# Projection tiles issued behind each batch of an S5 scan, and eight gate tiles per layer computed there and kept in HBM

## The chip, the cores and the metric

One Trainium2 chip (trn2), one core of it. The metric is the device time of one execution in microseconds. The kernel before took a median of 1589.26 us in three runs (1584.7 to 1589.46). Its five engines are called PE (TensorE), DVE (VectorE), ACT (ScalarE), POOL (GpSimd) and SP (SyncE, which here issues nearly all DMAs).

## What is computed

One inference step of a two-layer backbone over 640 tokens (512 latent, 128 context) of width 1024. What matters here of one layer:

```python
h = rms_norm(x) * (1 + scale) + shift
u_a, g_a, u_b, g_b, u_c, g_c, m = split(h @ w_in)
y_a = s5_glu(u_a) * silu(g_a)          # 32 groups x 16 channels, scans in both directions
y_b = hyena(u_b) * silu(g_b)           # two long convolutions by FFT
y_c = multipool(u_c) * silu(g_c)       # centred means over 2, 4, 8, 16 positions
m_a, m_b, m_c = split(sigmoid(m))
merged = m_a * (y_a @ w_br_a) + m_b * (y_b @ w_br_b) + m_c * (y_c @ w_br_c)
x = x + gate * (merged @ w_out)
```

The combined projection `h @ w_in` has 56 column tiles of 128 columns. Of these 0 to 3 are u_a, 4 to 7 g_a, 8 to 19 u_b, 20 to 23 g_b, 24 to 27 u_c, 28 to 31 g_c, and 32 to 55 the merge gates of the three branches, eight each.

## The kernel before

**A projection tile.** `win(l, nt, cb)` computes one of the 56 tiles for all 640 tokens by `linear` (L248 to L259). Both operands are kept as a rounded high part and a low part, and three products make up one: for two weight chunks of 128 x 512, each loaded by SP (tile `wr`, three slots), ACT writes the high part `wh` (L234) and DVE the low part `wl` (L235). For both halves of 320 tokens and eight blocks of 128 rows PE runs three matmuls (L257, L258, L259), 48 in all, into one `mm` buffer of PSUM for each half (three slots). `cb(half, ps)` takes the finished half out of PSUM.

**Merge tiles in pairs.** The merge tiles of branches b and c (40 to 55) are computed two at a time by `win2`, with seven products of a 2 x 2 block scheme where the plain way has eight: 7 x 12 = 84 matmuls for two tiles (L329 to L331). It needs four weight loads, sums of weights on POOL (L314 to L317), seven weight splits, five additions on DVE and two on POOL (L335). Its prepared operands `thi` and `tlo` are made by `win2_prep` (L282), on DVE, during the merges of branch a.

**The order of one layer** in the program (`layer`, then `merges`):

1. `u_a`: four tiles, written to HBM and read back regrouped (`load_u`).
2. Eight batches of the S5 scan. `s5_gen` builds a batch's operands: tables on DVE, POOL and ACT, transposes (L864) and small products (L884) on PE, and a kernel `kd` that goes to HBM and comes back as `mt` in eight pieces. `s5_run` does PE products (L929, L931), the rotation and scans on DVE (L938 to L953, the scans are L946 and L947), output products on PE (L959, L961) and a GELU (L965 to L969) whose result goes to HBM.
3. Twelve Hyena input tiles (`conv_u`): a projection tile copied by ACT into a padded tile `raw` (two slots, L982), then a three-tap filter by one ACT (L987) and two DVE instructions (L989, L991).
4. Four gate tiles of branch b (`gate_b`): a projection tile with a Silu on ACT (L998), and a POOL product (L1006).
5. `glu`: four tiles of g_a, and the GLU of branch a.
6. Four Hyena calls (`hyena`). Each has a loop over four residues `r`: transform on PE (`xf`), products on DVE (L1101, L1102), sums on POOL (L1103, L1104), a split on ACT and DVE, and behind the loop the inverse transforms (L1117). Behind each call stands one `pool_branch`, with a projection tile of u_c (L1017) and one of g_c through `silu_tile` (tile `sgc`, L998), and behind the third and fourth call two merges of branch a each (`merge`: a plain projection tile with a Tanh, L1189, then `branch`, a product with `w_br` and an accumulation, L1211 and L1213).
7. `merges`: the other four merges of branch a, the preparation of `win2`, then for branches b and c four calls of `merge2`: one `win2` and two `branch` calls each. In layer 0 the modulation products of the next step (L400) stand between them.

**What sets the order on the engines.** The program is written in a tile framework with a scheduler of its own (`TileContext(nc, schedule_with_timeline_sim=True)`): it knows the buffers and the data, and orders each engine's instructions by a model of the time. Each engine then works off its queue in order; so does SP with its DMAs.

## Time and profile before

| | |
|---|---|
| three runs, us | 1584.7, 1589.26, 1589.46 |
| profiled execution: span from first to last instruction, us | 1583.7 |
| busy: PE, PE weight loads, DVE, ACT, POOL (share of the span) | 92%, 88%, 74%, 41%, 44% |
| mean granted TensorE clock | 0.951 |
| HBM read, written, MB | 150.12, 21.56 |

The profiled execution is given by its span, 1583.7 us; what lies around the span (start and end of the program) is not part of it, and the lowest of the three runs is 1.0 us above it. Busy times count an engine's own instructions, not its waits nor the issue of DMAs. The granted clock is the share of TensorE's full clock that it was given, 1.00 being 2.4 GHz. In the views "x" is a count, "<-" stands between what an instruction writes and what it reads, and an arrow behind an idle time names what ended it.

### The profile page before, as it was taken

The page shows a single profiled execution, that of the slowest core. Times are in us where ns is not written, and L with a number is a line of the kernel's source. Part 1 is how long each engine was busy: PE and PEld are TensorE (multiplying, and loading weights), DVE is VectorE, ACT ScalarE, POOL GpSimd, SP SyncE. Part 2 cuts the span into 40 slices and gives each one's busy share as a digit, 9 for nine tenths or more (in the row PEclk, how much of TensorE's full clock was granted, in tenths as well). Part 3 has the DMA queues.
Part 4 walks back from the last instruction along what each step waited for, and adds up shares of the span by engine and source line. Part 5 has one row for each costly group of instructions (what it writes and reads, how often), then busy time and mean ns, then how long its engine had stood idle before and what let it go on. Part 6 is the DMA issues. An engine that isn't in the chain of part 4 may idle for free.

```text
span 1583.7 us, 28484 instructions
## 1 busy us (share of the span) xinstructions
PE 1460.2 (92%) x10764; PEld 1390.7 (88%) x10764; DVE 1179.0 (74%) x1964; ACT 645.1 (41%) x1330; POOL 690.9 (44%) x704
## 2 busy tenths in 40 slices
PE   4888887899999999999998878889999999999997
PEld 2568887799999998999997878889999999999996
DVE  6689999965777795555677799998377769766565
ACT  3274333324333443444335543333443334444443
POOL 5926465630344325454322646654115243566411
PEclk8689888999999999999999998889999999999999
DMA  9425212234222334553552431222532213222154
GB/s 319 164 81 124 68 53 61 61 89 142 91 80 79 102 104 150 180 170 139 190 180 89 123 100 53 64 61 70 152 96 75 81 61 120 81 81 83 41 169 154
DMA packets 114945, 173.53 MB, mean 110 GB/s; under 512 B 30360, under 2 KB 54568, under 8 KB 114297
## 3 DMA queue, kind: packets, MB, share of 16 engines
q1 hardware_dynamic: 113433, 165.37, 33.4%
q0 software_dynamic: 1296, 6.19, 1.1%
q8 instruction: 85, 1.39, 0.3%
q14 instruction: 51, 0.42, 0.1%
q10 hardware_dynamic: 80, 0.16, 0.0%
HBM read 150.12 MB, written 21.56 MB: 108 GB/s over the span
## 4 chain that ended last, share of the span: by engine, by line
PE 64%; DVE 19%; issue 5%; POOL 4%; DMA 3%; SPq 2%; ACT 2%; POOLq 0%; DVEq 0%; ACTq 0%
PE mm L259 13%; PE mm L258 13%; PE mm L257 13%; PE mm L329 4%; PE mm L331 4%; PE mm L330 4%; DVE wl L235 2%; PE modp L400 2%; DVE i L854 1%; PE inva L1117 1%; PE invb L1117 1%; DVE i L853 1%; DVE vx L989 1%; DVE kk L947 1%; DVE kk L946 1%
## 5 line engine op out<-in xcount | busy, mean ns | idle before, releaser
L257 PE MATMUL mm<-hhi,wh 128*128 128x320 f32 x1280 | 405.1, 318 | 10.8 <-ACT raw L982 6.9
L259 PE MATMUL mm<-hhi,wl 128*128 128x320 f32 x1280 | 404.9, 319 | 9.5 <-DVE wl L235 9.4
L258 PE MATMUL mm<-hlo,wh 128*128 128x320 f32 x1280 | 404.7, 317 | 4.4 <-DVE hlo L661 3.6
L235 DVE TENSOR_TENSOR wl<-wr,wh 128x512 fp32r<-128x512 f32 x312 | 256.2, 823 | 90.1 <-ACT wh L234 86.7
L234 ACT CAST wh<-wr 128x512 fp32r<-128x512 f32 x312 | 192.6, 618 | 250.6 <-PE mm L258 181.2
L257 PEld LDWEIGHTS mm<-hhi,wh 128*128 128x128 f32 x1280 | 247.2, 193 | 14.4 <-ACT raw L982 7.9
L259 PEld LDWEIGHTS mm<-hhi,wl 128*128 128x128 f32 x1280 | 246.8, 193 | 12.9 <-DVE wl L235 11.9
L258 PEld LDWEIGHTS mm<-hlo,wh 128*128 128x128 f32 x1280 | 247.5, 193 | 6.5 <-DVE hlo L661 4.5
L258 PE MATMUL mm<-mlo,wh 128*128 128x320 f32 x256 | 79.7, 312 | 0.5 <-DVE mlo L238 0.4
L329 PE MATMUL mm<-hhi,wh 128*128 128x320 f32 x256 | 79.9, 312 | 0.0
L331 PE MATMUL mm<-hhi,wl 128*128 128x320 f32 x256 | 79.5, 311 | 0.0
L257 PE MATMUL mm<-mhi,wh 128*128 128x320 f32 x256 | 79.0, 312 | 0.5 <-ACT wh L234 0.5
L259 PE MATMUL mm<-mhi,wl 128*128 128x320 f32 x256 | 78.9, 310 | 0.4 <-DVE wl L235 0.4
L330 PE MATMUL mm<-hlo,wh 128*128 128x320 f32 x256 | 79.2, 309 | 0.0
L235 DVE TENSOR_TENSOR wl<-ws,wh 128x512 fp32r<-128x512 f32 x64 | 54.4, 849 | 32.1 <-ACT wh L234 30.8
L1211 DVE SCALAR_TENSOR_TENSOR mth<-mth,mm 128x320 f32<-128x320 f32 x64 | 31.2, 488 | 54.8 <-PE mm L259 54.8
L234 ACT CAST wh<-ws 128x512 fp32r<-128x512 f32 x64 | 39.7, 620 | 72.8 <-PE mm L330 36.9
L335 DVE TENSOR_TENSOR mth<-mm,mth 128x320 f32<-128x320 f32 x80 | 39.2, 491 | 33.8 <-PE mm L331 17.2
L961 PE MATMUL yp<-w,ow 128*128 128x81 f32 x256 | 45.5, 307 | 17.5 <-DVE w L953 17.4
L331 PE MATMUL mm<-thi,wl 128*128 128x320 f32 x192 | 60.7, 316 | 0.0
L329 PE MATMUL mm<-thi,wh 128*128 128x320 f32 x192 | 60.6, 316 | 0.0
L330 PE MATMUL mm<-tlo,wh 128*128 128x320 f32 x192 | 59.4, 309 | 0.0
(420 smaller groups left out, 4069.0 us busy)
## 6 DMA issues: line engine op xcount, KB each, us to landing
wr<-w_in SPq DMA_DIRECT2D x224, 256.0 KB
wm<-w_mod SPq DMA_DIRECT2D x48, 512.0 KB
wr<-w_out SPq DMA_DIRECT2D x48, 256.0 KB
hd<-hs SPq DMA_DIRECT2D x32, 256.0 KB
hsr<-hd SPq DMA_DIRECT2D x32, 256.0 KB
mt<-kd SPq DMA_DIRECT2D x128, 32.0 KB
wr<-w_br_a SPq DMA_DIRECT2D x16, 256.0 KB
wr<-w_br_b SPq DMA_DIRECT2D x16, 256.0 KB
```

What stands on the lines that cost most here:

```text
L234: nc.scalar.copy(hi, src)
L235: nc.vector.tensor_tensor(out=lo, in0=src, in1=hi.bitcast(F32), op=ALU.subtract)
L257: nc.tensor.matmul(ps[i], wh[:, ks], at(hi, k, sl), start=(k == 0), stop=False)
L258: nc.tensor.matmul(ps[i], wh[:, ks], at(lo, k, sl), start=False, stop=False)
L259: nc.tensor.matmul(ps[i], wl[:, ks], at(hi, k, sl), start=False, stop=(k == kt - 1))
L329: nc.tensor.matmul(out, wh[:, ks], xh, start=(k == 0), stop=False)
L330: nc.tensor.matmul(out, wh[:, ks], xl, start=False, stop=False)
L331: nc.tensor.matmul(out, wl[:, ks], xh, start=False, stop=(k == 3))
L335: e.tensor_tensor(out=o, in0=x, in1=y, op=ALU.add)
L400: nc.tensor.matmul(ps[r0:r0 + 32, :], self.cs[:, 2 * hf + q, :], w[:, q, :], start=(hf < 2), stop=(hf >= 2))
L961: nc.tensor.matmul(yp[:, cols], ow[:, r, g].rearrange("p t h -> p (t h)"), w[:, r, g, 0:CW], start=False, stop=(r == 1))
L1117: nc.tensor.matmul(out, yy[:, ri, cs], ww, start=(n == 0), stop=(n == 5))
```

## The change

Behind each of the eight scan batches of a layer three projection tiles are issued, from a list `beside` in this order: the twelve Hyena tiles, the four gate tiles of branch b, four tiles 28 to 31 (g_c, Silu) and four tiles 40 to 43 (merge gates of branch b, Tanh of half the value). The last eight are new there. `ahead` computes such a tile by `win`, puts its activation into a slot of the tag `raw`, and stores it to a tile `gd` in HBM by an SP DMA of 320 KB. Where the tile was computed before, it is now read back by an SP DMA: in `silu_tile` for the pooling branch, and in `merge2` for its first two calls of branch b, which then call no `win2`. The order of the final-state DMA (`ns`) and the tiles changes accordingly.

```diff
--- before.py
+++ after.py
@@ -219,7 +219,7 @@
 class Body:
     def __init__(self, nc, tc, I, O, dbg=None):
         self.nc, self.tc, self.I, self.O, self.dbg = nc, tc, I, O, dbg or {}
-        self.smod, self.sacc = {}, {}
+        self.smod, self.sacc, self.gd = {}, {}, {}
 
     def dump(self, name, ap):
         if name in self.dbg:
@@ -991,8 +991,22 @@
         nc.vector.scalar_tensor_tensor(out=o, in0=raw[:, 2:644], scalar=cw[:, 3 * i + 2:3 * i + 3], in1=o,
                                        op0=ALU.mult, op1=ALU.add)
 
+    def ahead(self, l, nt, func, scale, U):
+        nc = self.nc
+        st = U.tile([P, L642 + 2], F32, tag="raw", name="gst", bufs=2)[:, 0:T]
+
+        def cb(half, ps):
+            nc.scalar.activation(st[:, half * HT:half * HT + HT], ps, func, scale=scale)
+
+        self.win(l, nt, cb)
+        self.gd[l, nt] = self.DR.tile([P, T], F32, name=f"gd{l}_{nt}")
+        nc.sync.dma_start(self.gd[l, nt], st)
+
     def silu_tile(self, l, nt, dst):
         nc = self.nc
+        if (l, nt) in self.gd:
+            nc.sync.dma_start(dst[:, 0:T], self.gd[l, nt])
+            return
 
         def cb(half, ps):
             nc.scalar.activation(dst[:, half * HT:half * HT + HT], ps, AF.Silu)
@@ -1193,7 +1207,12 @@
 
     def merge2(self, l, n, br, ys):
         ths = [self.M.tile([P, 644], F32, tag="t", name="mth", bufs=4)[:, 0:T] for _ in range(2)]
-        self.win2(l, 32 + 8 * br + n, ths)
+        nt = 32 + 8 * br + n
+        if (l, nt) in self.gd:
+            for i in range(2):
+                self.nc.sync.dma_start(ths[i], self.gd[l, nt + i])
+        else:
+            self.win2(l, nt, ths)
         for i in range(2):
             self.branch(l, n + i, br, ys, ths[i])
 
@@ -1370,14 +1389,16 @@
             uas = [SP.tile([P, NT, CW], F32, name=f"ua{i}") for i in range(2)]
             self.u_a(l, S, uas)
             self.load_u(l, S)
+            beside = [lambda i=i: self.conv_u(l, i, vx[i // 4][:, i % 4, :], SP) for i in range(12)]
+            beside += [lambda i=i: self.gate_b(l, i, S, vx[2]) for i in range(4)]
+            beside += [lambda i=i: self.ahead(l, 28 + i, AF.Silu, 1.0, SP) for i in range(4)]
+            beside += [lambda i=i: self.ahead(l, 40 + i, AF.Tanh, 0.5, SP) for i in range(4)]
             for b in range(NB):
                 g = self.s5_gen(l, b, S)
                 self.s5_run(l, b, S, g)
+                for _ in range(3):
+                    beside.pop(0)()
             nc.sync.dma_start(self.O['ns'][l], self.nst)
-            for i in range(12):
-                self.conv_u(l, i, vx[i // 4][:, i % 4, :], SP)
-            for i in range(4):
-                self.gate_b(l, i, S, vx[2])
         se.close()
         self.close = []
```

## Rows read from the trace of the kernel before

**Rows 1.** The page: span, and busy time of two engines.

```profile
span 1583.7 us, 28484 instructions
PE 1460.2 (92%) x10764; PEld 1390.7 (88%) x10764; DVE 1179.0 (74%) x1964; ACT 645.1 (41%) x1330; POOL 690.9 (44%) x704
```

**Rows 2.** Busy time by window (first row: the columns), stages around the change.

```profile
core 0: us, PE busy (x) PEld busy (x) DVE busy (x) ACT busy (x) POOL busy (x), PEclk, DMA share, GB/s
297.00:352.00 55.00, 52.30 (x487) 50.89 (x488) 42.39 (x59) 16.87 (x36) 21.24 (x22) 0.95 0.28 84
404.00:545.00 141.00, 140.11 (x1021) 138.51 (x1020) 101.73 (x194) 45.86 (x93) 55.93 (x73) 1.00 0.23 76
545.00:587.00 42.00, 42.00 (x289) 42.00 (x288) 41.34 (x80) 21.07 (x46) 12.53 (x5) 1.00 0.35 115
587.00:770.00 183.00, 183.00 (x1254) 166.45 (x1254) 101.83 (x169) 75.63 (x139) 88.19 (x76) 1.00 0.47 158
1165.00:1312.00 147.00, 146.12 (x1062) 144.51 (x1061) 106.78 (x205) 50.12 (x103) 56.00 (x73) 1.00 0.25 81
```

**Rows 3.** The same view of the two scan stages.

```profile
145.00:352.00 207.00, 177.88 (x1647) 169.78 (x1639) 188.43 (x260) 75.14 (x173) 111.10 (x87) 0.91 0.26 73
938.00:1120.00 182.00, 157.65 (x1435) 152.10 (x1435) 165.52 (x232) 63.82 (x146) 102.12 (x83) 0.88 0.21 62
```

**Rows 4.** Single lines, whole run: durations (least/median/most, ns), first and last start.

```profile
L982 ACT COPY raw<-mm x72: 242/316/435, 155.8 to 1074.2; 128x320 f32<-128x320 f32 x24, 128x192 f32<-128x192 f32 x24, 128x128 f32<-128x128 f32 x24
L946 DVE TENSOR_TENSOR_SCAN kk<-d,z x32: 805/826/2641, 166.7 to 1103.0; 64x328 f32<-64x328 f32 x32
L998 ACT ACTIVATE sgb<-mm x16: 428/434/439, 319.5 to 1118.2; 128x320 f32<-128x320 f32 x16
```

**Rows 5.** VectorE's instruction groups, 145 to 352 us: count, busy us, mean ns.

```profile
L235 DVE TENSOR_TENSOR wl<-wr,wh 128x512 fp32r<-128x512 f32 x32 | 27.6, 865 | 3.0 <-ACT wh L234 2.9
L991 DVE SCALAR_TENSOR_TENSOR vx<-raw,par,vx 128x642 f32<-128x642 f32 x12 | 13.1, 1095 | 0.2
L989 DVE SCALAR_TENSOR_TENSOR vx<-raw,par,vx 128x642 f32<-128x642 f32 x12 | 12.1, 1012 | 0.0
```

**Rows 6.** PE's projection matmuls, 297 to 352 us: first of three groups.

```profile
L257 PE MATMUL mm<-hhi,wh 128*128 128x320 f32 x80 | 25.2, 315 | 0.0
```

**Rows 7.** PE's projection matmuls, 145 to 352 us: first of three groups.

```profile
L257 PE MATMUL mm<-hhi,wh 128*128 128x320 f32 x257 | 83.2, 324 | 3.5 <-ACT raw L982 3.5
```

**Rows 8.** Instruction groups of the Hyena stage, whole run: count, busy us, mean ns.

```profile
L1101 DVE TENSOR_TENSOR m<-xf,hsr 128x512 f32<-128x512 f32 x32 | 22.0, 688 | 3.5 <-PE xf L547 2.2
L1102 DVE TENSOR_TENSOR m<-xf,hsr 128x512 f32<-128x512 f32 x32 | 21.8, 681 | 0.0
L1103 POOL TENSOR_TENSOR m<-m 128x256 f32<-128x256 f32 x32 | 24.5, 766 | 64.4 <-DVE m L1101 56.0 <-DMA wr<-w_in 5.7 <-ACT wh L234 2.7
L1104 POOL TENSOR_TENSOR m<-m 128x256 f32<-128x256 f32 x32 | 29.3, 916 | 2.0
L234 ACT CAST yh<-m 128x512 fp32r<-128x512 f32 x32 | 19.8, 620 | 50.0 <-POOL m L1104 49.8
L235 DVE TENSOR_TENSOR yl<-m,yh 128x512 fp32r<-128x512 f32 x32 | 23.8, 742 | 26.9 <-ACT yh L234 26.4
```

**Rows 9.** Waits, 120 to 350 us: who waited for whom, total us, times, longest.

```profile
PE yp L959 <- DMA mt<-kd: 6.8, 2, 3.9
```

**Rows 10.** Waits of SP's queue, 100 to 360 us, longest first.

```profile
SPq L248 <- DVE wl L235: 79.4, 26, 6.7
```

**Rows 11.** The chain that ended last, in order of time: start, us, what.

```profile
161.83 1.77 DMA mt<-kd
...
354.53 8.77 DMA yr<-yd
```

## The prediction

> **What bounds the kernel now.** I read the page's busy times first. TensorE (PE) works 1460.2 of 1583.7 us [rows 1], so the chip is short of matmul time, and a change that adds matmuls can gain only by filling holes in PE. The table by stage shows where the holes are. From the end of the scan to the merges PE has none: 140.11 of 141 us in the Hyena stage, 42.00 of 42 in the merges of branch a, 183.00 of 183 behind them, all at a granted clock of 1.00 [rows 2]. In the two scan stages (145 to 352 us for layer 0, 938 to 1120 for layer 1) PE is busy 177.88 of 207 and 157.65 of 182 us, at a clock of 0.91 and 0.88, and there VectorE (DVE) is the fuller engine, with 188.43 and 165.52 us [rows 3]. The stage is a contest of both.
>
> The merge window gives what a matmul of 320 columns takes at the full clock: 42.00 us / 289 = 0.145 us [rows 2]. A projection tile is 8 x 3 x 2 = 48 of them, 7.0 us.
>
> How the queues are ordered matters more here than the place in the program. The Hyena tiles' copies (L982) are issued behind all eight scans, yet run from 155.8 us, while the first layer's scans begin at 166.7 us and the second's end after 1103 us; only the gates (L998 sgb) stand at the end, from 319.5 us [rows 4]. So the schedule already pulls later work into a free engine, and the change mainly sets which work wins when both are ready, and puts eight tiles per layer where they can be pulled to.
>
> **The sum, per layer.** *Removed behind the scan:* four gate tiles of the pooling branch, 4 x 7.0 = 28.0 us of PE in the Hyena stage; two calls of the seven-product routine for merge tiles 40 to 43, 7 x 12 = 84 matmuls each, 2 x 84 x 0.145 = 24.4 us. Both lie where PE is full [rows 2], so PE's queue shrinks there by 52.4 us. With the two calls go 14 weight splits, their ScalarE copies, ten DVE and twelve GpSimd additions. They run beside a full PE; I count them as nothing, and if that cover went, they would be a gain, not a cost.
>
> *Added in the scan stage:* eight tiles, 8 x 7.0 = 56 us of PE and 16 weight splits of 0.865 us = 13.8 us of DVE [rows 5]. How much of the 56 us the stage absorbs is the main term. Between 297 and 352 us PE ran 487 matmuls in 52.30 us [rows 2], 239 of them projections (three groups of 80, 80 and 79) [rows 6]: 34.7 us. The other 248, of the scan batches, took 17.6 us, 0.071 each. In 145 to 352 us there were 770 projections (257, 257 and 256) among 1647 [rows 3, 7]: a need of 770 x 0.145 + 877 x 0.071 = 174 us of the 207. With the tiles it is 230; DVE's is 188 + 14 = 202. PE becomes the bound of the stage. At 100% it would last 230 us, 23 longer than now; with nothing absorbed 56 longer. I take the rate of the window nearest to the new mix, 297 to 352 us, where tiles without DVE work behind them already run beside scans: 52.30 of 55, 95%. 230 / 0.95 = 242, **35 us longer**.
>
> A check by halves: behind the first four batches stand all twelve Hyena tiles. Half the scans' DVE time ((188.4 - 27.6 - 13.1 - 12.1) / 2 = 68 us) and 12 x (2 x 0.865 + 1.095 + 1.012) = 46 [rows 5] make 114 us of DVE, and PE wants 12 x 7.0 + 31 = 115 us as well. Behind the last four, PE wants the same 115 and DVE only 68 + 21 = 89. So no half can do better than PE, and the first has both engines full; 95% is nearer to the good end than to the bad one.
>
> *Hyena stage:* it loses 28 us of cover. Its own chain is serial: for each of four residues of a call, product (0.688), product (0.681), difference (0.766) and sum (0.916) on GpSimd, cast (0.620), low part (0.742) [rows 8], 4.4 us, 4 x 4 x 4.4 = 71 us for four calls, and transposes, folds and inverse transforms come on top. DVE's need is 101.73 less 8 x 0.7 for the splits that leave, 96 us; PE's is 140 - 28 = 112, both below 141 [rows 2]. Between a stage that shrinks by all 28 us (loss 0) and a chain that cannot shrink at all (loss 28), I take a **loss of 8 us**: nearer to the first, since the pooling tiles and four merges still cover it. The merges after it can't make up for it: DVE is at 41.34 of 42 us there [rows 2], with the preparation of the seven-product routine.
>
> *DMA and waits:* eight stores of 320 KB and eight loads per layer go onto SP's queue; sixteen weight loads of 256 KB only move, past the S5 batches' own transfers. A store waits for the second half's activation; behind it on SP stand the next weight load and a later batch's kd, mt and yd transfers, and PE's scan products wait for mt (6.8 us in two waits now) [rows 9]. SP already stands 79.4 us for weight slots in this stage [rows 10], so it has room. The nearest price of a store and load through HBM is between 1.77 and 8.77 us [rows 11]; the load's use is tens of us away, so I take **1 us** per layer, with 0 and 12 (three batches late by the longest wait, 3.9 us) as ends. The store holds one of two `raw` slots; the next user is two tiles, 14 us, later. The activations (16 halves, Silu and Tanh) only move; ScalarE is idle for over half of either stage.
>
> Per layer: -52.4 + 35 + 8 + 1 = -8.4 us; both layers **-17 us**, 1% of the time. The profiled span is 1583.7 us; the median of the three runs is 1589.3, 5.6 us above it (the lowest, 1584.7, is 1.0 above). The difference is worked out in the span and taken off the median: **1572 us**.
>
> **The rivals.**
> *A, both covers hold.* The scan stage packs PE to 100% (23 us) and Hyena shrinks by its whole 28 us: -52.4 + 23 = -29.4 per layer, **1530 us**. For it: PE shows 100% in every later stage. Against it: never beside the scans.
>
> *B, the Hyena chain is left bare.* Place: 404 to 545 and 1165 to 1312 us. If the chain, not PE, paces this stage, all 28 us are lost: -52.4 + 35 + 28 + 1 = +11.6 per layer, **1612 us**. It decides from a loss of 16.4 us on: a stage that comes out less than 12 us shorter makes the kernel slower. For it: 71 us of the chain are certain, and PE's 100% hides how long the rest is. Against it: PE needs 112 us there, and the four merge tiles behind can be pulled in.
>
> *B2, with the clock.* Where PE had holes, its clock was 0.91 and 0.88; where it had none, 1.00 [rows 2, 3]. The clock has two levels, 2.4 and 1.2 GHz; 0.9 is a mix of them, and at it 112 us of matmuls would take 12 us more, per layer: **1636 us**. The Trainium skill ("TensorE: Matmul & The Clock Gate", Part 1: The HAM clock gate) says that idleness throttles the array to half its rate until it is busy again. By that rule, which the scan stages bear out, a bare Hyena chain costs clock too, and a filled scan stage wins some back.
>
> *C, the change doesn't do what it says.* The order on the engines isn't the program's [rows 4]. As the four gates stand at the end of the scan now, half of the eight tiles may end up behind the last scan with nothing beside them: the stage grows by the middle between 35 and 56, 45 us. -52.4 + 45 + 8 + 1 = +1.6 per layer, **1592 us**.
>
> **How the numbers follow.** A measurement of this kernel can tell about 0.3%, 4.8 us, from no change. Forecast (net gain of some 5 to 45 us) 0.48; A 0.12; B 0.13; B2 0.05; C 0.22, two thirds of it within 0.3%. Faster: 0.48 + 0.12 = 0.60; same 0.15; slower 0.13 + 0.05 + 0.07 = 0.25. The forecast's own range, with the scan stage 27 to 40 us longer and the Hyena loss 3 to 10, is 1546 to 1586. The range of 8 in 10 reaches down to near A and up to the weaker cases of B: 1535 to 1606.
>
> **What the new profile would show.** Right: the scan stage (first scan to last gate or tanh tile) some 35 us longer, PE at 9 of 10 or more in it with a clock near 1.00, silu and tanh tiles between the scans of batches 5 to 7; a Hyena stage some 20 us shorter with PE a little under full; 24 us less in the merges of branch b; and 48 matmuls more over the run. Wrong: a scan stage over 50 us longer with the moved tiles behind the last scan (C); holes before the Hyena products with GpSimd's or DVE's chain as releaser (B), at a clock under 1.00 (B2); waits of PE for mt or for the read-back tiles, which I priced at 1 us.

## The result, and the profile after

The changed kernel takes a median of 1605.22 us (four runs, 1602.55 to 1613.5), beside 1589.3 us for the kernel before on the same chip: a ratio of 1.0114, 95% interval 1.0085 to 1.0144. It is **slower by some 16 us**. The forecast was 1572 us and faster; the measured time lies at the upper end of the range of 1535 to 1606, on the other side of the kernel before. The profiled execution spans 1601.3 us against 1583.7, 17.6 more.

The page of after, in the place of [rows 1], and below it the bytes moved:

```profile
span 1601.3 us, 28515 instructions
...
PE 1471.1 (92%) x10812; PEld 1396.9 (87%) x10812; DVE 1145.4 (72%) x1932; ACT 632.5 (40%) x1310; POOL 649.0 (41%) x680
...
HBM read 155.36 MB, written 26.80 MB: 114 GB/s over the span
```

PE runs exactly the 48 matmuls more that were forecast (10812 for 10764). Read and written bytes grow by 5.24 MB each, 16 tiles of 320 KB. But PE is busy 10.9 us longer, where 48 matmuls of 0.145 us make 7.0: some matmuls became slower. And the span grew by more than the busy time: PE also idles longer.

To see where, I cut both executions at the same events: the first scan of a layer, the first sga activation (the GLU begins), the first residue product, the end of the last Hyena call, the last merge of branch a, and the first update of the residual X (the merges of branches b and c lie before it).

| stage, us | before, layer 0 | after | before, layer 1 | after |
|---|---|---|---|---|
| scan stage, first scan to first sga | 190.7 | 228.5 | 185.2 | 229.6 |
| GLU | 55.3 | 53.6 | 55.8 | 54.0 |
| Hyena calls | 132.2 | 123.1 | 132.2 | 126.1 |
| rest of the merges of branch a | 44.3 | 45.4 | 44.3 | 45.4 |
| merges of b and c | 188.8 | 165.3 | 162.6 | 138.8 |

What lies outside (the start, and from X to the next layer's first scan or to the end) differs by 3 us at most. The GLU, the Hyena calls and the rest of branch a are best read as one stretch, for tiles run across their borders: 231.8 to 222.2 us in layer 0, 232.4 to 225.5 in layer 1 (before: 1123.1 to 1355.5 us). So per layer: the scan stage pays 37.8 and 44.4 us, the merges give 23.5 and 23.8, and the stretch from which 28 us of TensorE work were taken gives **9.6 and 6.9**.

The busy time by window, first of the kernel before at those events (columns as in [rows 2]; scan stage, the stretch's three parts in layer 0, then scan stage and stretch of layer 1):

```profile
166.70:357.30 190.60, 163.14 (x1494) 155.62 (x1493) 171.61 (x238) 67.11 (x152) 104.63 (x88) 0.90 0.22 65
357.30:412.60 55.30, 55.06 (x378) 54.40 (x378) 32.47 (x50) 26.70 (x51) 2.46 (x6) 1.00 0.42 127
412.60:544.80 132.20, 131.31 (x961) 130.08 (x961) 95.74 (x184) 43.39 (x87) 53.55 (x67) 1.00 0.23 76
544.80:589.10 44.30, 44.30 (x304) 44.30 (x304) 43.61 (x84) 22.17 (x48) 12.61 (x6) 1.00 0.34 111
938.00:1123.10 185.10, 160.75 (x1456) 155.20 (x1456) 166.22 (x233) 64.44 (x147) 103.73 (x88) 0.88 0.22 66
1123.10:1355.50 232.40, 230.77 (x1640) 228.89 (x1639) 171.84 (x318) 92.04 (x186) 68.72 (x78) 1.00 0.30 94
```

and of the kernel after (scan stage, GLU, the four Hyena calls, rest of the merges; then layer 1):

```profile
163.80:392.30 228.50, 214.72 (x1893) 209.91 (x1892) 179.10 (x261) 87.79 (x193) 98.85 (x88) 0.96 0.32 94
392.30:445.90 53.60, 49.64 (x333) 48.83 (x332) 26.81 (x42) 18.89 (x39) 2.46 (x6) 0.97 0.29 86
445.90:479.20 33.30, 29.24 (x188) 27.26 (x187) 23.56 (x45) 10.48 (x22) 16.81 (x21) 0.90 0.24 76
479.20:512.70 33.50, 32.34 (x234) 31.65 (x234) 24.20 (x50) 9.68 (x19) 11.81 (x18) 1.00 0.25 77
512.70:539.30 26.60, 22.65 (x160) 21.89 (x160) 21.18 (x43) 9.04 (x18) 14.82 (x17) 0.90 0.29 87
539.30:569.10 29.80, 29.80 (x212) 29.48 (x212) 19.48 (x40) 8.41 (x16) 9.81 (x11) 0.97 0.18 54
569.10:614.50 45.40, 45.40 (x312) 45.40 (x311) 44.80 (x89) 22.25 (x48) 12.01 (x4) 1.00 0.43 138
940.60:1170.20 229.60, 211.99 (x1864) 207.10 (x1863) 178.71 (x256) 85.81 (x192) 97.05 (x88) 0.96 0.31 93
1170.20:1395.70 225.50, 210.11 (x1426) 205.34 (x1425) 161.54 (x306) 78.57 (x162) 66.35 (x77) 0.95 0.28 89
```

*The scan stage.* PE was idle for 190.60 - 163.14 = 27.5 us of it before, and for 13.8 after; its busy time grew by 51.6 us, a little less than the 8 x 7.0 = 56 that were added, beside a granted clock that rose from 0.90 to 0.96. Half of the holes were filled, and the rest of the work made the stage longer. Part of the growth lies behind the last scan: from its end to the first sga activation it is now 25.5 and 25.8 us, and was 21.1 and 16.8.

*The stretch behind it.* Before, PE was idle for 1.1 of 231.8 us (55.06 + 131.31 + 44.30 = 230.67), all at a clock of 1.00. After, its six windows hold 209.07 us of work in 222.2: idle for 13.1. And the clock is 0.90 in two of the four calls, 0.97 in the GLU. That is the whole account of layer 0: of 28.0 us of work taken out, 12.0 came back as idle time and, the busy time having shrunk by 21.6 only, 6.4 as matmuls at a lower clock; 9.6 are left. In layer 1 idle time grew from 1.6 to 15.4 us (225.5 - 210.11), and 6.9 are left. (Counted by their starts, 212 and 213 matmuls fewer lie in the stretch, where 192 were taken out: some 20 now fall outside its two cuts. At 0.145 us they are some 3 us, so by this estimate the stretch itself returned rather 7 and 4 us, and the clock's share of the loss is larger.) The clock's two levels are 2.4 and 1.2 GHz. The granted clock was below 1.00 in the three windows in which PE idled for some 4 us each, and in the one right behind the last of them; in the second call, with 1.2 us of idle time, it was 1.00.

Who PE waited for in this stretch (layer 0: what waited, for which releaser, us in total, times, longest):

```profile
PE zt L1088 <- DVE zc L555: 4.0, 1, 4.0
PE xf L545 <- ACT zh L234: 2.0, 2, 1.1
PE inva L1131 <- DVE hpm L1149: 1.9, 1, 1.9
PE inva L1131 <- DVE yl L235: 1.9, 2, 1.1
PE inva L1131 <- ACT yh L234: 1.8, 1, 1.8
PE xf L545 <- DVE m L1116: 1.0, 1, 1.0
PE xf L546 <- DVE zl L235: 0.4, 1, 0.4
```

Before, the same view has 0.9 us for the pooling product and 0.2 us. After there is no single large wait. The longest comes just before the first Hyena call's products: the transposes (`zt`) that stand next in PE's queue are those of the second call, issued ahead, and wait 4.0 us until DVE's fold (`zc`) has read the first call's, for `zt` has one buffer. The others are up to 1.9 us each, at the casts and low parts of a residue and at the combining of the inverse parts (`hpm`): links of the calls' own chain, with no projection tile in front of them in PE's queue.

The moved tiles themselves (activation and store; least/median/most in ns, first and last start):

```profile
L999 ACT ACTIVATE gst<-mm x32: 418/433/446, 318.5 to 1164.7; 128x320 f32<-128x320 f32 x32
L1003 SPq DMA_DIRECT2D gd<-gst x16: 326/327/362, 324.4 to 1165.2; - x16
```

The activations run from 318.5 to 386.9 us in layer 0, beside and behind the last three of the eight batches: the last scan ends at 366.8 us, so two of the eight tiles, and the second half of a third, stand behind it (in layer 1 as well). No wait of any engine names the tensor `gd` as its releaser: the read-back through HBM cost nothing that shows. SP's queue stood 10.1 us per layer, 2.7 at the longest, in front of the stores. PE's wait for `mt` (rows: before and after in layer 0, before and after in layer 1):

```profile
PE yp L959 <- DMA mt<-kd: 6.8, 2, 3.9
PE yp L959 <- DMA mt<-kd: 5.1, 3, 3.2
PE yp L959 <- DMA mt<-kd: 2.9, 1, 2.9
PE yp L959 <- DMA mt<-kd: 6.3, 3, 3.6
```

Over both layers it grew from 9.7 to 11.4 us.

### The profile page after: what moved, and what is told of

Its sections match the earlier page's. It is cut to its first block, busy times and chain, and to the rows that moved or that the text cites. A ratio compares the mean times of both kernels' runs of the same rounds, so it can differ in the third digit from the quotient of the medians.

```text
span 1601.3 us, 28515 instructions
## 1 busy us (share of the span) xinstructions
PE 1471.1 (92%) x10812; PEld 1396.9 (87%) x10812; DVE 1145.4 (72%) x1932; ACT 632.5 (40%) x1310; POOL 649.0 (41%) x680
## 4 chain that ended last, share of the span: by engine, by line
PE 67%; DVE 19%; issue 5%; POOL 3%; ACT 3%; DMA 2%; SPq 1%; POOLq 0%; DVEq 0%; ACTq 0%
PE mm L258 14%; PE mm L259 14%; PE mm L257 14%; PE mm L329 3%; PE mm L331 3%; PE mm L330 3%; DVE wl L235 2%; PE modp L400 2%; PE yp L961 2%; DVE vx L991 1%; DVE i L853 1%; PE invb L1131 1%; PE inva L1131 1%; DVE kk L947 1%; DVE i L854 1%
## 5 line engine op out<-in xcount | busy, mean ns | idle before, releaser
L257 PE MATMUL mm<-hhi,wh 128*128 128x320 f32 x1408 | 444.2, 317 | 4.8 <-ACT raw L982 3.5
L259 PE MATMUL mm<-hhi,wl 128*128 128x320 f32 x1408 | 440.3, 315 | 8.8 <-DVE wl L235 8.7
L258 PE MATMUL mm<-hlo,wh 128*128 128x320 f32 x1408 | 443.3, 315 | 4.1 <-DVE hlo L661 3.3
L259 PEld LDWEIGHTS mm<-hhi,wl 128*128 128x128 f32 x1408 | 269.5, 192 | 11.0 <-DVE wl L235 10.7
L257 PEld LDWEIGHTS mm<-hhi,wh 128*128 128x128 f32 x1408 | 269.3, 192 | 9.3 <-ACT raw L982 4.2
L258 PEld LDWEIGHTS mm<-hlo,wh 128*128 128x128 f32 x1408 | 269.9, 192 | 7.6 <-DVE hlo L661 4.7
L1232 POOL TENSOR_TENSOR macc<-macc,mth 128x320 f32<-128x320 f32 x32 | 34.8, 1094 | 85.5 <-DVE mth L1230 85.5
L329 PE MATMUL mm<-hhi,wh 128*128 128x320 f32 x192 | 59.9, 312 | 0.0
L331 PE MATMUL mm<-hhi,wl 128*128 128x320 f32 x192 | 59.4, 309 | 0.0
L330 PE MATMUL mm<-hlo,wh 128*128 128x320 f32 x192 | 59.4, 309 | 0.0
L855 POOL TENSOR_TENSOR i<-i,i 128x1024 f32<-128x1024 f32 x16 | 42.6, 2663 | 35.2 <-DVE i L853 19.2
L961 PEld LDWEIGHTS yp<-w,ow 128*128 128x128 f32 x256 | 40.2, 223 | 19.1 <-DVE w L953 19.1
L1232 POOL TENSOR_TENSOR acc<-acc,mth 128x320 f32<-128x320 f32 x32 | 37.7, 1178 | 44.4 <-DVE mth L1230 44.3
```

The source lines that it names most:

```text
L257: nc.tensor.matmul(ps[i], wh[:, ks], at(hi, k, sl), start=(k == 0), stop=False)
L258: nc.tensor.matmul(ps[i], wh[:, ks], at(lo, k, sl), start=False, stop=False)
L259: nc.tensor.matmul(ps[i], wl[:, ks], at(hi, k, sl), start=False, stop=(k == kt - 1))
L329: nc.tensor.matmul(out, wh[:, ks], xh, start=(k == 0), stop=False)
L330: nc.tensor.matmul(out, wh[:, ks], xl, start=False, stop=False)
L331: nc.tensor.matmul(out, wl[:, ks], xh, start=False, stop=(k == 3))
```

## Experiments

Four groups: what each part is worth, what the Hyena stretch lacks, what the order in the scan stage does, and which tiles are worth moving. "Cover" is other work that PE can do while a chain of dependent steps runs on other engines. Stage times in the text are cut at the same events as above.

### Take the work away, move nothing

The kernel before with a part of its work left out: first the four gate tiles of branch c (ones in their place), then the first two seven-product calls of branch b (a constant in the place of these four merge gates).

```diff
-        self.silu_tile(l, 28 + i, sg)
+        nc.gpsimd.memset(sg[:, 0:T], 1.0)
```

> The kernel before, with the four g_c gate tiles of the pooling branch left out of the Hyena stage (28 us of PE per layer gone, nothing added elsewhere; ones stand in their place). Theory H (the Hyena chain sets the pace once that cover is gone; in the changed kernel the stage became 6 to 9 us shorter): 10 to 20 us faster than before for both layers, 1570 to 1580 us. Rival P (PE is the bound, the chain follows): 50 to 56 us faster, 1533 to 1539 us.

```diff
-        self.win2(l, 32 + 8 * br + n, ths)
+        if br == 1 and n < 4:
+            for i in range(2):
+                self.nc.gpsimd.memset(ths[i], 0.5)
+        else:
+            self.win2(l, 32 + 8 * br + n, ths)
```

> The kernel before, with the first two seven-product calls of branch b left out of both layers (constants in place of the four gates). Theory H: PE is the bound there, so the whole 2 x 24.4 us go: 45 to 50 us faster than before, about 1541 us. Rival (the modulation products of layer 0 or DVE's preparation become the bound): 20 to 35 us faster.

Without the gate tiles: 1571.9 us (1571.14 to 1573.51), ratio 0.9884 (0.9847 to 0.9920). Of 56 us of TensorE work only 17 come back, with nothing added anywhere; the stretch itself shrank by 8.4 and 2.8 us. Without the two calls: 1542.86 us, ratio 0.9691 (0.9647 to 0.9736): of 2 x 24.4 us of work 46 come back. Both came as theory H had them: one half of the change takes from a place that returns a third, the other from a place that returns nearly all.

### One half of the change alone

```diff
             beside += [lambda i=i: self.ahead(l, 28 + i, AF.Silu, 1.0, SP) for i in range(4)]
-            beside += [lambda i=i: self.ahead(l, 40 + i, AF.Tanh, 0.5, SP) for i in range(4)]
...
-                for _ in range(3):
+                for _ in range(3 if b < 4 else 2):
```

> The change with the four Silu tiles alone moved (three tiles behind each of the first four batches, two behind the others; the Tanh tiles stay with the seven-product routine). Theory H: the scan stage grows by 15 to 25 us per layer, the Hyena stage shrinks by 6 to 9: 15 to 30 us slower than before, at or above the changed kernel, 1603 to 1620 us. Rival S (the loss is the scan stage's alone, and is shared by all eight tiles alike): about half of the changed kernel's loss, 1595 to 1599 us.

and, with the other of the two lines taken out:

> The change with the four Tanh tiles alone moved (the Silu tiles stay in the pooling branch and cover the Hyena chain). Theory H: scan stage 15 to 22 us longer per layer, merges 24 us shorter, Hyena as before: 4 to 20 us faster than before, 1570 to 1585 us. Rival S: about half of the changed kernel's loss, 1595 to 1599 us.

The silu tiles alone: 1613.08 us, ratio 1.0142 (1.0102 to 1.0182), by the medians slower than the whole change, though the two intervals overlap. The scan stage pays 11.9 and 15.5 us for them, the stretch behind gives back 3.5 in layer 0 and takes 1.3 in layer 1. The tanh tiles alone: 1568.81 us, ratio 0.9855 (0.9814 to 0.9897): the scan stage pays 10.8 and 16.2, the merges give 23.5 and 23.8. The times came as theory H had them (the second 1 us below its range), the stages not quite: the scan stage paid less than its 15 us in one case each, and the Hyena stretch gave less than its 6 to 9. The scan stage pays about the same for four tiles of either kind; what decides is what is bought with it.

### The new order without any moved tile

The sixteen tiles of before, two behind each batch.

```diff
+            beside = [lambda i=i: self.conv_u(l, i, vx[i // 4][:, i % 4, :], SP) for i in range(12)]
+            beside += [lambda i=i: self.gate_b(l, i, S, vx[2]) for i in range(4)]
...
+                for _ in range(2):
+                    beside.pop(0)()
             nc.sync.dma_start(self.O['ns'][l], self.nst)
-            for i in range(12):
-                self.conv_u(l, i, vx[i // 4][:, i % 4, :], SP)
-            for i in range(4):
-                self.gate_b(l, i, S, vx[2])
```

> The order alone: the sixteen tiles of before, two behind each batch, no tile moved, nothing stored. Theory H: the new order by itself costs or gains little, since the schedule fills by itself: scan stage within 5 us per layer of before, total within 10 us of it, 1579 to 1599 us. Rival O (issuing tiles ahead of the next batch delays the scan chain): 15 to 30 us slower, 1604 to 1619 us.

1585.78 us, ratio 0.9973 (0.9945 to 1.0001): no difference. The Hyena tiles already ran between the scans [rows 4], so issuing them there changed nothing.

### What the Hyena stretch lacks: the chain through the residues?

The sums on GpSimd (L1117 and L1118 in after) are the slowest link between a residue's product and its cast [rows 8]. I moved them to DVE, in after and in before, and then left them out of both (the residues' products then go on without the complex sum).

```diff
-            nc.gpsimd.tensor_tensor(out=m1[:, 0], in0=m1[:, 0], in1=m1[:, 1], op=ALU.subtract)
-            nc.gpsimd.tensor_tensor(out=m1[:, 1], in0=m2[:, 0], in1=m2[:, 1], op=ALU.add)
+            nc.vector.tensor_tensor(out=m1[:, 0], in0=m1[:, 0], in1=m1[:, 1], op=ALU.subtract)
+            nc.vector.tensor_tensor(out=m1[:, 1], in0=m2[:, 0], in1=m2[:, 1], op=ALU.add)
```

> The changed kernel with the two sums of each Hyena residue (0.77 and 0.92 us on POOL) made by VectorE, which takes about half as long: the chain of a residue gets about 0.8 us shorter, 16 residues per layer, VectorE has room there (90.9 of 130 us). Theory H (the chain sets the pace when bare): 5 to 12 us per layer come back, 10 to 24 us faster than the changed kernel, 1581 to 1595 us. Rival (DVE or psum buffers set the pace): within 5 us of the changed kernel.

> The same edit in the kernel before. Theory H: PE is full there, so a shorter chain gains nothing: within 5 us of before, 1584 to 1594 us. Rival (the chain sets the pace there too, and PE's 100% only follows): 10 to 24 us faster, 1565 to 1579 us.

1612.97 us in after (ratio to before 1.0152, 1.0095 to 1.0208, where the change has 1.0114) and 1596.89 in before (1.0044, 1.0014 to 1.0074): 0.4% slower in before; in after the difference is as large, but the intervals overlap. Both expectations missed. Each sum became faster (766 and 916 ns on GpSimd in before, [rows 8]; here DVE in after):

```profile
L1117 DVE TENSOR_TENSOR m<-m 128x256 f32<-128x256 f32 x16 | 8.8, 552 | 0.0
L1118 DVE TENSOR_TENSOR m<-m 128x256 f32<-128x256 f32 x16 | 8.1, 505 | 0.3
```

Yet the four calls of after grew from 123.1 and 126.1 us to 130.8 and 130.2. That DVE, which also serves the splits of this chain, then had too much to do (102.02 us of work in the calls of layer 0, where it had 88.42) is likely, but not shown.

```diff
-            nc.gpsimd.tensor_tensor(out=m1[:, 0], in0=m1[:, 0], in1=m1[:, 1], op=ALU.subtract)
-            nc.gpsimd.tensor_tensor(out=m1[:, 1], in0=m2[:, 0], in1=m2[:, 1], op=ALU.add)
```

> The changed kernel with the two POOL sums of each Hyena residue left out (the split takes the first product as it is): 1.7 us less in the chain of a residue, 16 residues per layer, no engine gets more work, PE's work stays the same. Theory H (the bare chain sets the pace): the Hyena stage gets 10 to 25 us shorter per layer and the kernel 15 to 45 us faster than the changed one, 1560 to 1590 us. Rival (VectorE's queue or the order of PE's work, not the chain, sets the pace): within 8 us of the changed kernel.

> The same sums left out of the kernel before. Theory H: PE is full in its Hyena stage, a shorter chain has nothing to give: within 6 us of before, 1582 to 1594 us. Rival (the chain paces the stage there as well): 15 to 45 us faster.

After without the sums: 1600.04 us, a ratio to before of 1.0054 (1.0025 to 1.0083) for 1.0114 with them: 5 us less by the medians, some 9 by the ratios. The calls got much shorter (123.1 to 105.8 us and 126.1 to 107.8), but the rest of the merges grew by 12.5 and 13.1. The stretch became 3.9 and 4.7 us shorter in all. Its three windows in layer 0:

```profile
397.20:451.60 54.40, 50.45 (x330) 49.38 (x329) 26.84 (x42) 18.88 (x39) 2.46 (x6) 0.94 0.29 85
451.60:557.50 105.90, 98.57 (x707) 95.50 (x706) 82.82 (x171) 33.84 (x69) 25.89 (x35) 0.97 0.24 76
557.50:615.40 57.90, 57.57 (x393) 57.31 (x392) 49.26 (x96) 25.73 (x56) 5.81 (x4) 1.00 0.41 126
```

218.2 us with 206.59 of work: 11.6 us idle, where after has 13.1 (layer 1: 12.4 for 15.4). The chain's slowest link is gone, and most of the holes are still there; the calls' gain was largely lost in the merges behind them. Before without the sums took 1583.95 us (ratio 0.9955, 0.9924 to 0.9986), where the calls shrank by 17.8 us and the rest of the merges grew by 16.6 in layer 0: there PE is full, and the whole stretch became only 0.3 and 1.8 us shorter, though the kernel as a whole is 0.45% faster, by a little more than the 6 us of theory H. In after the calls shrank as theory H had it, but the kernel gained within the 8 us of the rival: that the GpSimd sums are what the removed tiles had covered is not borne out.

### Or the place of the other work?

Two merges of branch a stand behind the third Hyena call and two behind the fourth. Here one stands behind each call.

```diff
-                        if o == 1:
-                            for n in range(hf * NPRE // 2, (hf + 1) * NPRE // 2):
-                                self.merge(l, n, 0, (yahi, yalo))
+                        self.merge(l, 2 * o + hf, 0, (yahi, yalo))
```

> The changed kernel, but with one merge of branch a behind each of the four Hyena calls instead of two behind the third and two behind the fourth; the same work in all. Theory F (what the Hyena stage lacks is other TensorE work at the place of its holes, the starts of the calls 1 and 2): the stretch from the first glu activation to the last merge of branch a comes from 222 and 226 us to 205 to 214, and the kernel takes 1575 to 1592 us. Theory R (the chain through the residues sets a call's period, and other work beside it changes nothing): that stretch stays within 4 us in each layer, and the kernel within 7 us of 1605.

1600.54 us (ratio to before 1.0082, 1.0052 to 1.0112). The stretch takes 222.8 and 220.9 us, 0.6 more and 4.6 less than in after: theory F missed, theory R is near in its numbers. Layer 0, GLU, four calls, rest of the merges:

```profile
396.40:450.00 53.60, 49.64 (x333) 48.84 (x332) 26.81 (x42) 18.85 (x39) 2.47 (x6) 0.97 0.29 86
450.00:478.40 28.40, 26.71 (x198) 26.21 (x198) 21.82 (x44) 11.03 (x22) 12.20 (x13) 1.00 0.31 94
478.40:509.60 31.20, 31.20 (x231) 30.77 (x232) 23.97 (x49) 10.41 (x21) 12.93 (x18) 1.00 0.24 72
509.60:547.30 37.70, 34.20 (x226) 32.99 (x226) 24.75 (x50) 10.34 (x21) 15.17 (x21) 0.91 0.25 72
547.30:579.90 32.60, 28.05 (x179) 26.50 (x178) 20.75 (x42) 6.40 (x13) 16.29 (x18) 0.90 0.18 58
579.90:619.20 39.30, 39.30 (x270) 39.30 (x270) 38.22 (x75) 20.49 (x45) 8.19 (x5) 1.00 0.47 148
```

The second call is now full (31.20 of 31.20 us, at clock 1.00), the first nearly (26.71 of 28.40), both faster than in after (33.30 and 33.50). But the third and fourth idle for 3.5 and 4.5 us at a clock of 0.91 and 0.90, and the 4.0 us before the first call are there as well: 13.7 us idle in all. The holes moved to the calls that lost their cover. So neither the slowest link alone nor the place of the merges is the whole cause. What these runs show is this: in every run whose Hyena stretch lacks the four gate tiles, PE idles there for 11.6 to 19.0 us (after 13.1 and 15.4, the last run 13.7 in both layers, the kernel before with the gates left out 13.9 and 14.8); in every run that has them, for 0.6 to 3.8 (before 1.1 and 1.6).

### The order in the scan stage

All 24 tiles issued behind the eight batches, to see whether the scheduler pulls the moved ones forward by itself as it did the Hyena tiles:

```diff
-                for _ in range(3):
-                    beside.pop(0)()
             nc.sync.dma_start(self.O['ns'][l], self.nst)
+            for f in beside:
+                f()
```

> The changed kernel with all 24 tiles issued behind the eight batches, as the sixteen were before; the eight moved ones still stored and read back. Theory H (the place in the program matters little, the schedule fills by itself; the loss is the moved Silu tiles'): within 10 us of the changed kernel, 1595 to 1615 us. Rival O (the place behind each batch is what costs): 10 to 30 us faster than the changed kernel.

1646.5 us, ratio 1.0342 (1.0294 to 1.0390); the scan stage pays 57.6 and 58.7 us, the whole of the added work. Neither theory had expected that. The moved tiles' first activation and a window of the stage's end:

```profile
L999 ACT ACTIVATE gst<-mm x32: 430/437/491, 356.7 to 1210.6; 128x320 f32<-128x320 f32 x32
```

```profile
360.00:414.40 54.40, 53.32 (x364) 53.01 (x363) 16.12 (x24) 20.73 (x39) 0.00 (x0) 1.00 0.48 149
```

PE is nearly full, DVE works 16.12 of 54.4 us: a tail without scans. The Hyena tiles were pulled between the scans [rows 4], these were not; why, was not tried. The place behind each batch does matter for them.

If the place matters, so does the order within the list. In the change all twelve Hyena tiles, which have two DVE instructions of about a microsecond each behind them [rows 5], come first. The two parts of after's scan stage in layer 0 show it, the first with both engines busy, the second with PE alone full:

```profile
145.00:300.00 155.00, 141.24 (x1202) 137.03 (x1201) 141.88 (x209) 61.25 (x140) 80.70 (x65) 0.94 0.28 77
300.00:384.00 84.00, 83.03 (x779) 81.87 (x778) 47.67 (x68) 26.40 (x57) 24.73 (x29) 1.00 0.41 123
```

Here the Hyena tiles take turns with the others, which have no such instructions:

```diff
-            beside = [lambda i=i: self.conv_u(l, i, vx[i // 4][:, i % 4, :], SP) for i in range(12)]
...
+            beside = [f for p in zip(conv, more + gate) for f in p]
```

> The changed kernel with its 24 tiles in another order: a Hyena tile and a moved tile or gate by turns, so that VectorE's filters and the tiles without them are spread over all eight batches. Theory I (part of the scan stage's growth comes from its two halves, the first full on VectorE with 141.9 of 155 us, the second on PE with 83.0 of 84 us): scan stage 5 to 12 us shorter per layer, 10 to 24 us faster than the changed kernel, 1581 to 1595 us. Rival (PE's need of 230 us sets the stage in any order): within 6 us of the changed kernel.

1583.41 us (ratio 0.9957, 0.9925 to 0.9989): 22 less than after, by nothing but the order of a list. The time came as theory I had it, but out of other parts: the scan stages shrank by 14.7 and 15.8 us, more than its 5 to 12, and the stretch behind took some of it back. The scan stages of both layers, to be held against the 228.50 and 229.60 us above:

```profile
165.40:379.20 213.80, 207.46 (x1883) 203.47 (x1882) 177.09 (x258) 82.99 (x187) 94.93 (x88) 0.98 0.31 91
934.00:1147.80 213.80, 206.24 (x1859) 201.58 (x1858) 177.40 (x257) 81.95 (x184) 95.09 (x88) 0.98 0.30 88
```

Idle time fell to 6.3 and 7.6 us, the clock rose to 0.98. The stretch behind now gives back only 0.9 and 2.5 us against before. With both orders changed, turns in the scan stage and a merge behind each call:

> All eight moved tiles with both orders changed: conv tiles by turns with the moved ones in the scan stage (alone: 1583 us), and one merge of branch a behind each Hyena call. Theory F with O: both gains add up, 1550 to 1572 us, with a scan stage of 212 to 216 us and glu to last merge of branch a 205 to 214 us in each layer. Theory R: only the first gain is there, 1578 to 1590 us.

1576.39 us (ratio 0.9924, 0.9886 to 0.9962), between the two theories: the stretch takes 226.8 and 224.3 us, 4.1 and 5.6 less than with the turns alone. By these windows the place of the merges is worth something, but far from the 28; in the time, the intervals with and without it overlap.

### Which four tiles?

If the scan stage has 27.5 us of idle PE, it may have room for four tiles (28 us), not for eight. First more of the tanh kind, six in the change's order (three seven-product calls replaced), then four tanh tiles by turns, six tanh tiles by turns, and four silu tiles by turns.

```diff
-            beside += [lambda i=i: self.ahead(l, 28 + i, AF.Silu, 1.0, SP) for i in range(4)]
-            beside += [lambda i=i: self.ahead(l, 40 + i, AF.Tanh, 0.5, SP) for i in range(4)]
+            beside += [lambda i=i: self.ahead(l, 40 + i, AF.Tanh, 0.5, SP) for i in range(6)]
...
-                for _ in range(3):
+                for _ in range(3 if b < 6 else 2):
```

> Six Tanh tiles moved per layer (40 to 45, three calls of the seven-product routine replaced), no Silu tile. Theory H with the scan stage filling up: the first four tiles cost the scan stage 11 to 16 us per layer; two more cost 8 to 14 us and save 12.2 us: within 5 us of e4, 1563 to 1575 us. Rival (the scan stage still has room as for the first four): a third more gain than e4, 1557 to 1562 us.

The four tanh tiles by turns (`conv` are the twelve Hyena tiles; the two runs behind it differ in the moved tiles alone):

```diff
...
+            more = [lambda i=i: self.ahead(l, 40 + i, AF.Tanh, 0.5, SP) for i in range(4)]
+            more += [lambda i=i: self.gate_b(l, i, S, vx[2]) for i in range(4)]
+            beside = [f for i in range(4) for f in (conv[i], more[i])] + conv[4:8]
+            beside += [f for i in range(4) for f in (conv[8 + i], more[4 + i])]
...
-                for _ in range(3):
+                for _ in range(3 if b < 4 else 2):
```

> The four tanh tiles alone (no silu tile moved), with their order by turns with the conv tiles, so that the scan stage has a tile of mostly TensorE work and one of mostly VectorE work behind each batch. Theory O (the order is what the scan stage loses): with the convs first, four tanh tiles cost the scan stage 10.5 and 16.2 us in the two layers; by turns they cost under 6 each, and the kernel takes 1548 to 1562 us (with the convs first it took 1569). Rival A (the order only matters where eight more tiles stand at the end): scan stage as with the convs first, 200 us or more in both layers, 1563 to 1573 us.

> Six tanh tiles (three of the seven-product calls of branch b) by turns with the conv tiles, no silu tile. With the convs first, six took 1565 us, with a scan stage of 213 us and merges of b and c of 155 and 127 us. Theory O: the scan stage comes to 198 to 205 us, the merges stay at 155 and 127, the kernel takes 1535 to 1553 us and is the fastest of all. Rival A: scan stage 210 us or more, 1558 to 1568 us.

> The four silu tiles alone, by turns with the conv tiles, no tanh tile moved: the same 28 us of TensorE work per layer goes into the scan stage as in the four tanh tiles by turns (1544 us), but it is taken from the Hyena stage, not from the merges of branch b. Theory V (the scan stage has room for four tiles whatever they are, and the Hyena stage returns only a third of what is taken from it): scan stage 190 to 197 us, glu to the last merge of branch a 4 to 12 us shorter than before in each layer, 1562 to 1583 us. Rival S (moving the silu tiles costs by itself, by their stores, their read-back or their place): 1590 to 1613 us, as with the convs first.

| moved, per layer | median us | ratio to before | scan stage, us | GLU to last merge of a | merges b, c |
|---|---|---|---|---|---|
| none (before) | 1589.3 | | 190.7, 185.2 | 231.8, 232.4 | 188.8, 162.6 |
| 4 tanh, Hyena tiles first | 1568.81 | 0.9855 (0.9814 to 0.9897) | 201.5, 201.4 | 234.3, 231.1 | 165.3, 138.8 |
| 4 tanh, by turns | 1544.0 | 0.9743 (0.9698 to 0.9789) | 191.1, 192.6 | 231.1, 230.5 | 165.3, 138.8 |
| 6 tanh, Hyena tiles first | 1564.57 | 0.9842 (0.9796 to 0.9887) | 213.4, 212.2 | 230.6, 230.4 | 155.2, 126.5 |
| 6 tanh, by turns | 1549.59 | 0.9757 (0.9721 to 0.9793) | 204.1, 203.5 | 231.7, 232.1 | 155.2, 126.5 |
| 4 silu, by turns | 1578.57 | 0.9950 (0.9933 to 0.9966) | 190.9, 190.6 | 225.9, 225.5 | 186.8, 162.7 |
| 8, by turns | 1583.41 | 0.9957 (0.9925 to 0.9989) | 213.8, 213.8 | 230.9, 229.9 | 165.3, 138.8 |

The ratios stand to the kernel before on the same chip, whose medians were 1586 to 1591 us. Six tanh tiles in the change's order came within 5 us of four, as expected. Four tanh tiles by turns are the fastest kernel of the study that does the whole work, 42 us faster than before. (Its profiled run, with a span of 1553.8 us, began its scans 11.7 us later than that of before, ahead of everything that was edited; the three timed runs lie between 1541.43 and 1544.44.) Its scan stage in both layers:

```profile
178.40:369.50 191.10, 180.22 (x1691) 175.42 (x1691) 169.22 (x250) 75.14 (x171) 98.33 (x88) 0.98 0.29 84
924.50:1117.10 192.60, 181.56 (x1671) 177.25 (x1671) 169.68 (x249) 73.88 (x169) 99.39 (x88) 0.96 0.28 80
```

Layer 0 holds 28 us more of matmul work in 0.4 us more time: idle time fell from 27.5 to 10.9 us, and at a clock of 0.98 for 0.90 the busy time grew by 17.1 only. Theory O held, with 7.4 us in layer 1 for the 6 at most that it had put, and a time 4 us below its range. In kernels whose scan stage was not touched, layer 1's takes 183.6 to 190.2 us (185.2 in before) and layer 0's 190.5 to 191.1, so a few us in layer 1 tell little. Four silu tiles cost the stage as little (0.2 and 5.4 us), and the stretch behind them:

```profile
357.90:583.80 225.90, 211.11 (x1445) 206.31 (x1444) 166.11 (x311) 84.08 (x170) 69.42 (x78) 0.97 0.30 94
1119.30:1344.80 225.50, 211.81 (x1446) 207.10 (x1445) 165.25 (x312) 84.12 (x170) 69.74 (x78) 0.96 0.30 94
```

225.9 us with 211.11 of work, 14.8 idle; in layer 1 13.7. With the scan term nearly out of the way, the 28 us taken from here return 5.9 and 6.9. Theory V held: the same work placed in the same holes gives 1544 us when it is taken from the merges, and 1579 when it is taken from the Hyena stretch.

Two tiles more than four cost the scan stage 13.0 and 10.9 us, four more 22.7 and 21.2: 5.3 to 6.5 us a tile, nearly its 7.0 us of PE. The third seven-product call returns 10.1 and 12.3 us for its two tiles, so six are no better than four. Stages and time of six by turns came as theory O had them, but not that they would be the fastest: by the medians four are, and the intervals overlap.

## Why the prediction was wrong

Point by point, in its own steps, both layers:

- **PE is full behind the scan and has holes in it** [rows 2, 3]: right, and it was the right place to look.
- **The two seven-product calls, 24.4 us per layer**: right, 23.5 and 23.8 measured; no gain from the 14 weight splits that went with them shows, as taken.
- **The scan stage, 35 us longer**: 37.8 and 44.4. The term was mis-sized by 12 us in all, most of it in layer 1, which I had not worked out by itself: its stage was 5.5 us shorter than layer 0's before and is as long after (untouched, layer 1's stage varies by up to 6.6 us from kernel to kernel, so not all of this need be the change's). The 95% of PE that I took from 297 to 352 us came out as 94% and 92% (214.72 of 228.5, 211.99 of 229.6), so the rate was about right.
- **The check by halves** told more than I made of it. It said that with the Hyena tiles first the first half has both engines full and the second only PE. That is what happened (141.24 us of PE and 141.88 of DVE in 155, then 83.03 and 47.67 in 84). The cost of it was left out of the sum: the turns took 14.7 and 15.8 us off the stage. I had written that the schedule pulls later work into a free engine anyway; the run with all tiles behind the batches shows that it doesn't for the moved tiles.
- **The Hyena stage loses 8 us of its 28**: this is the step that failed. The losses were 18.4 and 21.1 us. It makes 23.5 of the some 35 us by which the two spans' difference was missed (17 shorter forecast, 17.6 longer measured), and by itself it crosses the 16.4 us from which rival B was to decide. I had placed the value near the good end "since the pooling tiles and four merges still cover it"; the windows show that they don't fill the stretch: PE idled there for 13.1 and 15.4 us, where it had idled for 1.1 and 1.6, and the busy time shrank by less than the work. Leaving the tiles out of the kernel before, with nothing added, gave the same picture: 17 us for 56.
- **DMA and waits, 1 us**: about right. No wait names the read-back, and PE's wait for `mt` fell by 1.7 us in layer 0 and grew by 3.4 in layer 1, 1.7 more over both.

**The rivals.** B's mechanism decided, in part and with part of B2's: cover was taken from a stage whose own chain can't fill PE, and some 6 of the 18.4 us of layer 0 are a busy time that shrank by less than the work, beside a lower granted clock. That B's 1612 us comes so near the measured 1605 is partly luck: its loss of 28 us per layer was 16.5 too large over both, its scan term 12.2 too small. The Trainium skill ("TensorE: Matmul & The Clock Gate", Part 1: The HAM clock gate), that idleness throttles the array, agrees with the windows: 1.00 in before, where PE had next to no holes, 0.90 in the two calls of after with 3.9 and 4.1 us of them. A was far off. C, the moved tiles behind the last scan, happened to two and a half of the eight tiles, not to half of them as it had put; the stretch behind the last scan grew by 4.4 and 9.0 us. What it costs in full is shown by the run that issued all tiles at the end: 57.6 and 58.7 us.

**What stays open.** Which link of the Hyena calls the missing cover exposes. Leaving out the GpSimd sums and moving the merges each left 11.6 to 13.7 us of idle time per layer; that an order of the calls exists without it was not shown, and neither was the opposite. In after the last merges of branch a, 45.4 us with PE full, stood behind the calls, though they take no data from them: whether they could be brought in front of the holes was not tried. Why the scheduler pulled the Hyena tiles between the scans and not the moved ones was not tried either; and the lower clock was only read beside the holes, never changed alone.

## What to carry to other kernels

What moving work into a hole is worth depends on two things: how much room the hole has, and how much the place that the work comes from really returns. Leaving the work out there, with nothing added, measures the second in one run (here 17 us for 56 of one kind, 46 for 49 of the other), and a fully busy engine doesn't answer it: PE was full in both places. When the room is limited, fill it with the tiles that buy most, and let those that need the other engine take turns with those that don't.

## What the runs showed that I had not expected

- The loads of 16 tiles of 320 KB back from HBM left no wait behind in the changed kernel. In the one with four tanh tiles per layer, which is 42 us faster, the stores held a DVE memset up by 0.7 us in all.
- Filling holes came with more clock: in the scan stage the granted clock rose from 0.90 to 0.98 with four tiles by turns, and 28 us of added work made the busy time only 17.1 us longer.
- Taking work away came with less clock: in two of the four Hyena calls it fell from 1.00 to 0.90, and 28 us less work shortened PE's busy time in the stretch by 21.6.
- Moving an instruction from GpSimd to a DVE with idle time to spare (before: 95.74 of 132.2 us busy in the calls) made the kernel before 0.4% slower, though each sum became faster. Of this the stretch shows 3.2 and 2.7 us; DVE's share in a stage didn't tell.
